# Expert MLP on one core: x of two experts loaded as 32 long rows, b1 from ScalarE, the first cast shared by two engines

## The chip, the core and the metric

One Trainium2 chip, one core. The metric is the time of one execution on the device, in microseconds (us). The runs of the kernel before took 181.45, 181.69 and 182.16 us; the median is 181.69. One further execution was recorded by the hardware profiler, and the lines below are from it.

## What is computed

Eight experts, each a two-layer perceptron on its own 256 rows of x. Everything comes in and goes out as fp32.

```python
def reference(x, w1, w2, b1, b2):   # x 8x256x512, w1 8x512x2048, w2 8x2048x512
    h = np.matmul(x, w1) + b1[:, np.newaxis, :]
    h = np.maximum(h, 0)
    return (np.matmul(h, w2) + b2[:, np.newaxis, :]).astype(np.float32)
```

One expert's w1 and w2 are 4 MB each in HBM, its x 512 KB and its result 512 KB.

## The kernel before

**Layout.** Weights and most of x are narrowed to fp16 by the DMA that loads them, which is issued by GpSimd. On the chip w1 of an expert is a tile of 128 partitions x 8192 fp16 (16 KB per partition), and so is w2. The contraction runs over partitions: rows of w1 are dealt out so that partition p holds rows 4p to 4p+3. x must therefore be transposed, and VectorE does that in blocks of 32x32 (`transposes`, lines 95 to 112): from a tile of rows t it writes xT, 128 partitions x (4 x 256) fp16. How many rows of x lie in one partition, R, decides the shape: with R = 2 an expert takes 16 instructions of 256 elements per partition (L109), with R = 4 it takes 16 of 256 (L112), with R = 8 it takes 8 of 512 (L112).

**Two products.** `first_product` (L114) makes 16 blocks of h transposed: for each, four matmuls (L121) into a PSUM tile `ph`, three of which exist, then ScalarE adds the bias from b1T and takes the maximum with 0 (L128), writing hT. In the middle of its 16 blocks it calls `transposes` for the next expert. xT has two buffers. `second_product` (L166) puts b2 into PSUM by a matmul with ones (L171), then adds 32 matmuls of hT and w2 (L178); VectorE copies one half of the result out (L156) and ScalarE the other (L157).

**Order.** The last loop (L227) runs step s = 0 to 10. At step s it puts in the DMAs that are due, runs the first product of expert s and the second product of expert s - 3 (LAG). All matmuls and all GpSimd DMAs are kept in program order. GpSimd's queue begins with w1 of expert 0, b2, b1, w1 of expert 1, x of experts 2 and 3, w1 of expert 2; the next, w1 of expert 3, must wait until the first product of expert 0 has given back its buffer, for w1 and w2 have three buffers each. From then on each load waits for such a buffer: w1 of expert 4 for the first product of expert 1, and so on. Results of experts 0 to 3 and of 4 and 5 are collected in two tiles and stored at the end by GpSimd; those of 6 and 7 are stored by SyncE and ScalarE.

**The start, which the change edits** (L187 to L211). x of experts 0 and 1 is not narrowed by its DMA. SyncE loads each as fp32 into a tile x32 of 128 partitions with two rows each (4 KB per partition), taken from the pool of result tiles. VectorE casts each to fp16 (L201), and after the first cast it transposes expert 0 (L109). b1 is loaded by GpSimd as 32 rows of 2 KB, and VectorE's four transposes at L208 make b1T out of it. They depend on b1's landing and stand, in VectorE's order, after seven of the sixteen transposes of expert 1. ScalarE's first instruction is the loading of its function table, followed by the first L128, which needs b1T.

Of the kernel before, what the change touches and what calls it, by code (L numbers as in the profile page):

```python
# [10 lines left out]
def kernel(  # L11
# [9 lines left out]
    nc = tc.nc  # L21
    fp32 = mybir.dt.float32
    fp16 = mybir.dt.float16
    E, T, H = x.shape
    M = w1.shape[2]
    P = 128
    nTB = T // P
    nKC = H // P
    nJ = M // P
    B = 32  # L30
    nB = P // B
# [9 lines left out]
    nXF32 = 2  # L41
    X_LOADS = {2: 2, 4: 4}

    def ordered(ins):
        return tc.keep_in_program_order(ins)
# [3 lines left out]
    w2_pool = ctx.enter_context(tc.tile_pool(name="w2", bufs=3))  # L49
    x_pool = ctx.enter_context(tc.tile_pool(name="xp", bufs=1))  # L50
# [3 lines left out]
    out_pool = ctx.enter_context(tc.tile_pool(name="outp", bufs=2))  # L54
# [5 lines left out]
    b1_rows = singles.tile([E * nB, M // nB], fp32)  # L60
    b1T = singles.tile([P, nJ * B + nB - 1], fp32)

    x16 = [None] * E
# [18 lines left out]
    def load_w1(e):  # L82
        w1_sb[e] = w1_pool.tile([P, nKC, M], fp16, tag="w1", name="w1sb")
        ordered(nc.gpsimd.dma_start(  # L84
            out=w1_sb[e], in_=w1[e].rearrange("(p kc) m -> p kc m", kc=nKC)
        ))
# [8 lines left out]
    def transposes(e):  # L95


        t, p0, R = x16[e]
        n = R // nTB
        xT[e] = xT_pool.tile([P, nKC, T], fp16, tag="xT", name="xT")  # L100
        for g in range(T // R // B):
            src = t[p0 + B * g : p0 + B * (g + 1)]
            for b in range(nB):
                block = src[:, :, b * (H // nB) : (b + 1) * (H // nB)].rearrange(
                    "p (n tb) (i kc) -> p tb kc n i", tb=nTB, kc=nKC)
                out = xT[e][b * B : (b + 1) * B].rearrange(
                    "p kc (tb g i n) -> p tb g kc n i", tb=nTB, i=B, n=n)
                if n == 1:
                    nc.vector.transpose(out=out[:, :, g, :, 0, :], in_=block[:, :, :, 0, :])  # L109
                    continue  # L110
                for tb in range(nTB):
                    nc.vector.transpose(out=out[:, tb, g], in_=block[:, tb])  # L112
# [71 lines left out]
                    ))  # L184
        store(e, po)

    x32 = []  # L187
    for e in range(nXF32):
        x32.append(out_pool.tile([P, nTB, H], fp32, tag="out", name="x32"))
        nc.sync.dma_start(out=x32[e], in_=x[e].rearrange("(p tb) h -> p tb h", tb=nTB))  # L190
    load_w1(0)
    ordered(nc.gpsimd.dma_start(  # L192
        out=b2_sb,
        in_=b2.rearrange("e h -> (e h)").rearrange("(o f) -> o f", o=1),
    ))
    ordered(nc.gpsimd.dma_start(out=b1_rows, in_=b1.rearrange("e (b i) -> (e b) i", b=nB)))  # L196
    nc.vector.memset(ones1, 1.0)  # L197

    for e in range(nXF32):
        t = x_pool.tile([P, nTB, H], fp16, tag=f"x{e}", name=f"x{e}")  # L200
        nc.vector.tensor_copy(out=t, in_=x32[e])  # L201
        x16[e] = (t, 0, nTB)
        if e == 0:
            transposes(e)


    for b in range(nB):
        nc.vector.transpose(  # L208
            out=b1T[b * B : (b + 1) * B, nB - 1 - b : nB - 1 - b + nJ * B],
            in_=b1_rows.rearrange("r (i j) -> r j i", j=nJ),  # L210
# [55 lines left out]
```

## Time and profile before

| what | value |
|---|---|
| median of three runs | 181.69 us |
| span of the profiled execution (no other time of it is given) | 179.7 us |
| median of the runs less that span | 2.0 us |
| TensorE matmuls busy | 129.1 us, 72% |
| VectorE busy | 88.0 us, 49% |
| ScalarE busy | 70.2 us, 39% |
| DMA | 40.56 MB landed or stored, mean 226 GB/s; 71.39 MB read from HBM, 4.19 MB written |
| GpSimd's queue (q0) | 3232 packets, 38.35 MB |
| SyncE's queue (q1) | 476 packets, 1.70 MB |
| ScalarE's queue (q10) | 112 packets, 0.39 MB |
| the two x32 loads | 512 KB each, issued at 0.74 and 1.17 us, landed 3.5 and 4.3 us after issue |
| first w1 load | issued at 1.25 us, landed 14.0 us later |
| b1 load | issued at 2.41 us, landed 13.2 us later |

How to read it: the span is cut into 40 slices of about 4.5 us, and a digit is the busy share of an engine in tenths. A matmul's end is modelled, since matmuls are pipelined. DMA bytes are counted on the side where a packet lands, so that a weight load that reads 4 MB counts as 2 MB. An instruction's line is that of the listing above. In a time line "idle before" is the time an engine stood still ahead of the instruction, with what ended the wait behind the arrow.

The start, by the time line: VectorE casts x of expert 0 at 4.26, transposes it from 5.11 to 12.29, casts x of expert 1 at 12.32, and transposes b1 from 16.19 to 20.37. TensorE begins at 15.28, when the first w1 has landed, and stops at 18.05, with all three PSUM tiles full, until ScalarE has b1T; it goes on at 22.28.

### The profile page before, as it was taken

How to read it: one execution, taken by the hardware profiler on the slowest of the kernel's cores; microseconds unless marked ns; L12 is line 12 of the kernel's file. 1: busy time of each engine (PE TensorE's matmuls, PEld its weight loads, DVE VectorE, ACT ScalarE, POOL GpSimd, SP SyncE). 2: the span in 40 equal slices, each digit the busy share in tenths (PEclk: the TensorE clock that was granted, in tenths of full speed). 3: DMA queues.
4: the chain of work that ended last, by engine and by line, in shares of the span. 5: the costliest groups of instructions: out<-in, count | busy, mean ns of one | idle time of the engine just before them, and what ended most of it. 6: DMA issues, size and time to landing. Idle time of an engine off the chain costs nothing.

```text
span 179.7 us, 1958 instructions
## 1 busy us (share of the span) xinstructions
PE 129.1 (72%) x784; PEld 85.8 (48%) x784; DVE 88.0 (49%) x125; ACT 70.2 (39%) x151; POOL 13.1 (7%) x28
## 2 busy tenths in 40 slices
PE   0005099969595970899969597969497887999950
PEld 0004079969592320795369244844195332433420
DVE  0999942987000199999999998003200020301010
ACT  0000459969593022483099005950586020020010
POOL 7000002120201010001010001000200021010000
PEclk9999999999998798589999889999999996999996
DMA  5999999999999999999999999999999999999996
GB/s 216 251 226 199 233 212 197 233 224 193 228 230 192 221 233 215 197 230 230 204 208 230 219 193 233 226 193 222 230 215 197 233 206 204 223 212 215 335 420 250
DMA packets 3829, 40.56 MB, mean 226 GB/s; under 512 B 461, under 2 KB 477, under 8 KB 1133
## 3 DMA queue, kind: packets, MB, share of 16 engines
q0 software_dynamic: 3232, 38.35, 96.6%
q1 hardware_dynamic: 476, 1.70, 2.4%
q10 hardware_dynamic: 112, 0.39, 0.5%
q8 instruction: 6, 0.10, 0.2%
q14 instruction: 3, 0.02, 0.0%
HBM read 71.39 MB, written 4.19 MB: 421 GB/s over the span
## 4 chain that ended last, share of the span: by engine, by line
DMA 66%; PE 26%; POOL 2%; another core or an unknown queue 1%; issue 1%; ACT 0%; POOLq 0%
DMA w1sb<-in_w_dram 44%; DMA w2sb<-in_w_dram 22%; PE po L178 18%; PE ph L121 8%; PE po L171 1%; POOL w1sb L84 1%; ACT out L157 0%; POOL x L76 0%; POOL b_sb L192 0%; POOL b_rows L196 0%; POOLq L250 0%
## 5 line engine op out<-in xcount | busy, mean ns | idle before, releaser
L121 PE MATMUL ph<-xT,w1sb 128*128 128x256 f16 x512 | 63.6, 289 | 34.8 <-DMA w1sb<-in_w_dram 23.9
L121 PEld LDWEIGHTS <-w1sb 128*128 128x128 f16 x512 | 59.0, 147 | 40.3 <-DMA w1sb<-in_w_dram 32.6
L178 PE MATMUL po<-w2sb,hT 128*128 128x512 f16 x256 | 61.4, 402 | 9.4 <-DMA w2sb<-in_w_dram 9.4
L112 DVE STREAM_TRANSPOSE xT<-x 32x256 f16<-32x256 f16 (+1 forms) x64 | 53.1, 889 | 25.6 <-DMA x<-in_x_dram 18.7
L128 ACT ACTIVATE hT<-ph,b1T 128x256 f16<-128x256 f32 x128 | 56.2, 474 | 13.6 <-PE ph L121 13.4
L178 PEld LDWEIGHTS <-hT 128*128 128x128 f16 x256 | 25.9, 102 | 44.7 <-issue 19.3
L156 DVE COPY out<-po 32x512 f32<-32x512 f32 (+2 forms) x22 | 15.1, 688 | 54.0 <-PE po L178 53.8
L157 ACT COPY out<-po 32x512 f32<-32x512 f32 (+2 forms) x22 | 12.7, 579 | 69.7 <-PE po L178 69.5
L109 DVE STREAM_TRANSPOSE xT<-x 32x256 f16<-32x256 f16 x32 | 14.0, 436 | 0.5
L93 POOL DMA_DIRECT2D w2sb<-in_w_dram x10 | 5.3, 534 | 72.8 <-PE po L178 72.8
L128 ACT ACT_TABLE_LOAD x1 | 1.3, 1283 | 20.5 <-DVE b1T L208 20.5
L84 POOL DMA_DIRECT2D w1sb<-in_w_dram x8 | 4.5, 558 | 63.2 <-PE ph L121 62.4
L171 PE MATMUL po<-b_sb,ones 1*128 1x512 f16 x16 | 4.8, 379 | 0.0
L208 DVE STREAM_TRANSPOSE b1T<-b_rows 32x512 f32<-32x512 f32 x4 | 4.1, 1035 | 0.1
L201 DVE CAST x<-x 128x1024 f16<-128x1024 f32 x2 | 1.5, 757 | 3.3 <-DMA x<-in_x_dram 3.3
L140 POOL DMA_DIRECT2D out_dram<-out x2 | 1.1, 542 | 10.9 <-ACT out L157 10.9
L171 PEld LDWEIGHTS <-ones 1*128 1x128 f16 x16 | 0.9, 92 | 2.1 <-issue 2.1
L76 POOL DMA_DIRECT2D x<-in_x_dram x2 | 1.1, 552 | 0.0
L197 DVE MEMSET ones<- 1x128 f16 x1 | 0.2, 165 | 0.8 <-PEq L250 0.8
L196 POOL DMA_DIRECT2D b_rows<-in_b_dram x1 | 0.5, 515 | 0.0
L192 POOL DMA_DIRECT2D b_sb<-in_b_dram x1 | 0.5, 513 | 0.0
L250 POOL MEMSET const-float32-0.0<- 128x1 f32 x1 | 0.1, 99 | 0.2 <-issue 0.2
(3 smaller groups left out, 0.3 us busy)
## 6 DMA issues: line engine op xcount, KB each, us to landing
w1sb<-in_w_dram POOLq DMA_DIRECT2D x8, 2048.0 KB, 34.5
w2sb<-in_w_dram POOLq DMA_DIRECT2D x6, 2048.0 KB, 46.8
w2sb<-in_w_dram POOLq DMA_DIRECT2D x4, 1024.0 KB, 24.0
out_dram<-out POOLq DMA_DIRECT2D x1, 2048.0 KB, 26.8
x<-in_x_dram SPq DMA_DIRECT2D x2, 512.0 KB, 3.9
x<-in_x_dram POOLq DMA_DIRECT2D x1, 1024.0 KB, 30.8
out_dram<-out POOLq DMA_DIRECT2D x1, 1024.0 KB, 17.8
x<-in_x_dram POOLq DMA_DIRECT2D x1, 512.0 KB, 24.0
```

The lines of the kernel that those rows point to most:

```text
L84: ordered(nc.gpsimd.dma_start(out=w1_sb[e], in_=w1[e].rearrange("(p kc) m -> p kc m", kc=nKC)))
L93: ordered(nc.gpsimd.dma_start(out=w2_sb[e][:, lo : lo + half], in_=src[:, lo : lo + half]))
L109: nc.vector.transpose(out=out[:, :, g, :, 0, :], in_=block[:, :, :, 0, :])
L112: nc.vector.transpose(out=out[:, tb, g], in_=block[:, tb])
L121: ordered(nc.tensor.matmul(out=ph, lhsT=w1_sb[e][:, kc, :].rearrange("p (q j) -> p q j", j=nJ)[:, :, j], rhs=xT[e][:, kc, :], start=(kc == 0),
L128: nc.scalar.activation(out=hT[e][:, j, :].rearrange("p (tb k i) -> p tb k i", tb=nTB, k=split), in_=ph.rearrange("p (tb i k) -> p tb k i", ...
L156: nc.vector.tensor_copy(out=out_sb[at : at + rows, k * nTB, :], in_=po[0][part])
L157: nc.scalar.copy(out=out_sb[at : at + rows, k * nTB + 1, :], in_=po[1][part])
L171: ordered(nc.tensor.matmul(out=t, lhsT=ones1, rhs=b2_sb[0:1, e * H : (e + 1) * H], start=True, stop=False,))
L178: ordered(nc.tensor.matmul(out=po[tb], lhsT=hT[e][:, j, tb * P : (tb + 1) * P], rhs=w2_sb[e][:, j, :], start=False, stop=(j == nJ - 1),))
L201: nc.vector.tensor_copy(out=t, in_=x32[e])
L208: nc.vector.transpose(out=b1T[b * B : (b + 1) * B, nB - 1 - b : nB - 1 - b + nJ * B], in_=b1_rows.rearrange("r (i j) -> r j i", j=nJ),)
```

## The change

SyncE loads x of experts 0 and 1 into one tile of 64 partitions, 32 for each expert, with eight rows of x (16 KB) in each partition. The tile comes from the pool of w2, not of results. ScalarE issues the load of b1 as its first instruction, in place of GpSimd. The fp16 copy is one tile x01 of the same layout. For expert 0 VectorE casts the first four rows of each partition and ScalarE the other four; expert 1 is cast by ScalarE alone. As R is now 8 for both, `transposes` takes 8 instructions of 512 elements for each, at L112, and L109 is no longer used.

```diff
-    x32 = []
+    RX = T // B
+    x32 = w2_pool.tile([nXF32 * B, RX, H], fp32, tag="w2", name="x32")
     for e in range(nXF32):
-        x32.append(out_pool.tile([P, nTB, H], fp32, tag="out", name="x32"))
-        nc.sync.dma_start(out=x32[e], in_=x[e].rearrange("(p tb) h -> p tb h", tb=nTB))
+        nc.sync.dma_start(out=x32[e * B : (e + 1) * B], in_=x[e].rearrange("(p r) h -> p r h", r=RX))
+    nc.scalar.dma_start(out=b1_rows, in_=b1.rearrange("e (b i) -> (e b) i", b=nB))
     load_w1(0)
     ordered(nc.gpsimd.dma_start(
         out=b2_sb,
         in_=b2.rearrange("e h -> (e h)").rearrange("(o f) -> o f", o=1),
     ))
-    ordered(nc.gpsimd.dma_start(out=b1_rows, in_=b1.rearrange("e (b i) -> (e b) i", b=nB)))
     nc.vector.memset(ones1, 1.0)
 
+    x01 = x_pool.tile([nXF32 * B, RX, H], fp16, tag="x01", name="x01")
     for e in range(nXF32):
-        t = x_pool.tile([P, nTB, H], fp16, tag=f"x{e}", name=f"x{e}")
-        nc.vector.tensor_copy(out=t, in_=x32[e])
-        x16[e] = (t, 0, nTB)
+        rows = slice(e * B, (e + 1) * B)
+        cut = RX // 2 if e == 0 else 0
+        if cut:
+            nc.vector.tensor_copy(out=x01[rows, :cut], in_=x32[rows, :cut])
+        nc.scalar.copy(out=x01[rows, cut:], in_=x32[rows, cut:])
+        x16[e] = (x01, e * B, RX)
         if e == 0:
             transposes(e)
```

The instructions are scheduled anew when the kernel is built. In the changed kernel VectorE's order at the start is: the memset of ones, the four transposes of b1, the cast of expert 0's half, eight transposes for expert 0, eight for expert 1, then expert 2 as before. ScalarE's is: the DMA issue, the table load, the half cast, the cast of expert 1, then the L128 blocks as before. TensorE's order is the same, and GpSimd's is the same without the load of b1.

## The prediction

> **What bounds the kernel now.** I began with the page's slices, to see which resource is never idle.
>
> ```profile
> PE   0005099969595970899969597969497887999950
> ...
> DMA  5999999999999999999999999999999999999996
> GB/s 216 251 226 199 233 212 197 233 224 193 228 230 192 221 233 215 197 230 230 204 208 230 219 193 233 226 193 222 230 215 197 233 206 204 223 212 215 335 420 250
> ```
>
> DMA is busy in all 40 slices; TensorE has gaps in most of them. The GB/s line counts bytes landed: weights arrive as fp16 at about 215, so about 430 are read, and the stores at the end run at 335 to 420 with nothing to narrow. The second view is the chain of waits, which says what the end hangs on.
>
> ```profile
> ## 4 chain that ended last, share of the span: by engine, by line
> DMA 66%; PE 26%; POOL 2%; another core or an unknown queue 1%; issue 1%; ACT 0%; POOLq 0%
> ```
> ```profile
> 4.00 34.57 DMA w1sb<-in_w_dram
> ...
> 110.12 39.38 DMA w2sb<-in_w_dram
> 149.50 0.04 issue
> 149.54 8.66 PE po L178 x32
> 158.20 0.53 PE po L171 x2
> 158.74 7.01 PE po L178 x32
> 165.75 0.53 PE po L171 x2
> 166.28 7.03 PE po L178 x32
> ```
>
> (Columns: start, duration.) The third weight load, put in at 4.00, lands at 38.57, because all that was queued before it goes first. So does w2 of expert 5: issued at 110.12, landed at 149.50. From there TensorE runs to 173.33 without a pause, and the last 512 KB store takes 4.8 us more. Whatever shifts the weight stream shifts the landing at 149.50, and with it the end, one for one. Work on VectorE or ScalarE counts only if it lets the GpSimd queue run dry.
>
> Third, the stream's first microseconds, since the change is there: the windows of half a microsecond (length, then busy time by engine, granted clock, DMA share, GB/s).
>
> ```profile
> 1.50:2.00 0.50, 0.00 (x0) 0.00 (x0) 0.00 (x0) 0.00 (x0) 0.50 (x2) 1.00 0.39 106
> 2.00:2.50 0.50, 0.00 (x0) 0.00 (x0) 0.00 (x0) 0.00 (x0) 0.50 (x2) 1.00 0.63 213
> 2.50:3.00 0.50, 0.00 (x0) 0.00 (x0) 0.00 (x0) 0.00 (x0) 0.50 (x2) 1.00 1.06 401
> 3.00:3.50 0.50, 0.00 (x0) 0.00 (x0) 0.00 (x0) 0.00 (x0) 0.50 (x2) 1.00 0.93 377
> 3.50:4.00 0.50, 0.00 (x0) 0.00 (x0) 0.00 (x0) 0.00 (x0) 0.50 (x1) 1.00 1.03 418
> 4.00:4.50 0.50, 0.00 (x0) 0.00 (x0) 0.24 (x1) 0.00 (x0) 0.50 (x2) 1.00 1.08 442
> ```
>
> These six move 0.5 x (106+213+401+377+418+442) = 978 KB. Weights can't come faster than about 215, so this is x, 1049 KB in all; the missing 70 KB at 442 take 0.16 us. **x occupies the engines from 1.5 to about 4.66, 3.16 us, and the weight stream stands behind it.**
>
> **The x load.** Bytes stay the same. 256 rows of 4 KB become 64 rows of 16 KB: on 16 engines, evenly spread, 4 packets each for 16. They go to 32 partitions per expert, 64 in all, where before each expert used 128. No row shows an uncast load to so few partitions, so I bound it. Low end: x's own best rows, 401, 377, 418 and 442, mean 410, from the first moment: 1049/410 = 2.56 us, that is 0.60 less than the 3.16 of now (the slow windows at 1.5 to 2.5 gone, with a quarter of the packets). High end: the row with packets of the same size. w1 rows are 16 KB in SBUF (128 x 8192 fp16), land at 213 GB/s at share 1.00 (window 22 to 24), and 16 of them take 262/213 = 1.23 us. Four packets per engine at that price are 4.92 us: 1.76 more than 3.16, or 2.36 more than the 2.56 of an undisturbed load. I take +1.6, near 1.76: the row with the same packet size is nearest, and a little may lie beside the first w1 packets, issued at 1.25, which can use an engine while another is held up by x. If that cover is complete, the cost is nothing.
>
> [...]
>
> **b1.** 64 KB leave the GpSimd queue, where at 426 read they cost 0.15 us, and one issue of 0.515 us goes from GpSimd. The 0.5 us by which w1 of expert 1 is put in sooner buys nothing: w1 of expert 0 is in flight until 15.28. The same 64 KB now go from ScalarE before x, while the DMA share is 0.39 or less: 0 to -0.15, taken as -0.1. ScalarE's issue (0.38 us in the ACTq row of the end) delays nothing; it did nothing until 20.45.
>
> **VectorE, ScalarE, TensorE.** New order on VectorE: memset, four b1 transposes, cast of half of x0, 8 transposes for expert 0, 8 for expert 1 (where 16 and 16 stood). They have the shape 32x512 of experts 4 to 7: 1331 ns by the grouped lines, for two of 436 before. So 8 x 1.331 = 10.6 us per expert, for 16 x 0.436 = 7.0.
> - b1 landed about as x0 does now (3.5 us after issue): 4.3. Transposes 4 x 1.035 = 4.1: 8.4.
> - x0 half on VectorE: 757 ns for 1024 elements, so 1.5 for 2048: 9.9. x0 landed meanwhile (4.3 now, plus at most 1.2).
> - ScalarE's share has no row; its 512-element copy of 579 ns, scaled, gives at most 2.3 for half of x0 and 4.6 for x1: done by 12.5, before VectorE needs either. The table load (1.28), which waited for b1T at 20.45, is done in ScalarE's idle start.
> - Transposes of x0: 20.5. The first product then runs from a cold clock: 9.78 for 64 matmuls (the product at 72.32, clock 0.50 in its first windows): ends 30.3. Now it starts at 15.28, stops at 18.05 for b1T, and ends at 30.2.
> - Transposes of x1: 31.1; second product 7.21: 38.3 (now 37.15). Transposes of expert 2: 16 of 0.43: 38.0, before its w1 lands (38.57, later by whatever x costs).
>
> So the wait for b1T goes, and longer transposes take its place; GpSimd's next loads, put in at 30.46 and 37.45 now, come at 30.4 and 38.4. The stream is covered until 38.57 by w1 of expert 2 already queued, so this is worth **0**. One wait is new: the load of w2 of expert 2 (issued at 46.65 now) needs x32's buffer, free since 12.5; behind it on GpSimd stand all later loads, none of which is held up. Out tiles no longer share with x32; nobody waits there.
>
> **Sum.** 179.7 + 1.6 - 0.1 = 181.2 of span. The page's execution has no time of its own beside its span; the median of the runs, 181.69, lies 2.0 above. 181.2 + 2.0 = **183.2 us**, 0.8% slower.
>
> **Rivals.**
> 1. *x's slowness is hidden, or isn't there.* While one engine writes x slowly, others read w1, or 16 KB rows land as fast as 4 KB ones. For it: x and w1 do overlap (4.50 to 5.00 shows 631 GB/s, more than either alone in any other window here). Against it: x has the engines nearly to itself before about 4.5. It decides if x costs under 0.9 us. Time: 179.7 + 0 to 0.8 + 2.0, about 181.8.
> 2. *The head of the stream gets shorter.* Mechanism: fewer packets fill the windows at 1.5 to 2.5 (lost there: 0.39 and 0.63 of full share, 0.5 us), at most -0.60, b1 -0.15. It decides if the early windows rise to 400 GB/s. Time: 179.7 - 0.75 + 2.0 = 180.95; to count as faster it must gain over 0.9, which even the whole of this doesn't reach, unless packets also cost less later.
> 3. *The GpSimd queue runs dry near 36.* If the first product ends late, w1 of expert 3 is issued late. Place: the load now issued at 30.46. w1 of expert 2 lands at 38.57; from an issue to full flow about 3 us pass (1.25 to about 4.5 for the first w1, beside x), so it costs from about 35 on, 1 us per us. My path says 30.4; it would need 5 us more, such as b1 landing at 9. For it: b1 stands in front of everything on VectorE. Against it: it is issued first, on a queue of its own. Time with 2 us dry: 185.2.
> 4. *The change doesn't shorten VectorE's start at all*: that is already in my sum, and worth nothing.
>
> **How the numbers follow.** Forecast (x costs 0.9 to 2.6): 0.58, at 183.2. Rival 1: 0.31. Rival 2: 0.06, of which 0.04 beyond 0.5%. Rival 3: 0.05. About 0.5% (0.91 us) is what a measurement here can tell from no change: faster 0.04, same 0.33 (rival 1 and the rest of rival 2), slower 0.63. The range leaves out rival 3, most of rival 2 and the last of the others: from 181.4 (-0.3) to 184.3 (+2.6: the +2.36 bound and 0.2 for the spread of runs). The forecast's own range is 182.6 to 184.3.
>
> **What would show it.** In windows of 0.5 us the x phase at about 213 GB/s instead of 400, reaching to 5.5 or later; the landings of w1 of expert 2 (38.57) and w2 of expert 5 (149.50) both later by the same 1 to 2 us, with the chain behind them unchanged; 32x512 transposes at 1.33 us; a first product that starts once, near 20.5, and ends near 30.3; ScalarE's casts over by 12.5. It is wrong if x is in by 4.7 and the two landings stay (rival 1), if they come sooner (2), or if a window between 34 and 40 has little DMA (3).

## The result, and the profile after

The changed kernel takes **183.54 us** (median of five runs, 183.39 to 183.72) against 181.69: a ratio of 1.0098, 95% interval 1.0084 to 1.0112. The forecast was 183.2, slower by 0.8%. The profiled execution has a span of 181.7 us, 2.0 more than before; its own time is 183.54.

First the chain of waits of the changed kernel (start, duration), beside the one of before.

```profile
3.48 37.05 DMA w1sb<-in_w_dram
40.53 0.03 issue
...
112.15 39.56 DMA w2sb<-in_w_dram
151.72 0.04 issue
151.76 8.65 PE po L178 x32
160.40 0.53 PE po L171 x2
160.94 7.01 PE po L178 x32
167.95 0.53 PE po L171 x2
168.48 7.03 PE po L178 x32
```

w1 of expert 2 lands at 40.53 in place of 38.57 (+1.96), w2 of expert 5 at 151.72 in place of 149.50 (+2.22), and everything behind it has its old length. The time was lost ahead of 40 us and never came back. The time line shows that it was lost much sooner: the first w1 lands at 17.36, before at 15.28 (+2.08).

Next the windows of half a microsecond in the head of the stream (DMA share and GB/s are the last two columns).

```profile
1.50:2.00 0.50, 0.00 (x0) 0.00 (x0) 0.00 (x0) 0.50 (x1) 0.50 (x2) 1.00 1.68 426
2.00:2.50 0.50, 0.00 (x0) 0.00 (x0) 0.00 (x0) 0.47 (x1) 0.50 (x2) 1.00 0.28 98
2.50:3.00 0.50, 0.00 (x0) 0.00 (x0) 0.00 (x0) 0.00 (x0) 0.50 (x2) 1.00 0.94 217
3.00:3.50 0.50, 0.00 (x0) 0.00 (x0) 0.00 (x0) 0.00 (x0) 0.50 (x2) 1.00 1.67 373
3.50:4.00 0.50, 0.00 (x0) 0.00 (x0) 0.00 (x0) 0.00 (x0) 0.50 (x2) 1.00 0.21 41
4.00:4.50 0.50, 0.00 (x0) 0.00 (x0) 0.00 (x0) 0.00 (x0) 0.04 (x1) 1.00 1.87 373
4.50:5.00 0.50, 0.00 (x0) 0.00 (x0) 0.00 (x0) 0.00 (x0) 0.00 (x0) 1.00 0.88 176
5.00:5.50 0.50, 0.00 (x0) 0.00 (x0) 0.00 (x0) 0.00 (x0) 0.00 (x0) 1.00 0.48 98
```

A packet counts whole in the window in which it starts, so 16 KB packets that start together make single windows jump; read the mean. The last six move 217, 373, 41, 373, 176 and 98 GB/s, 213 on average, where the kernel before moved about 410 from 2.5 to 4.5 us. DMA share stays high all the same (1.01 from 2.50 to 5.50, before 1.02 from 2.50 to 4.50): **the engines are busy but move half as much**. Busy share alone would not have shown the loss.

The queues from 1.50 to 6.00 us say who holds the engines: packets, MB, and the time that the packets took as a share of 16 engines. q1 is SyncE's queue and brings x, q10 is ScalarE's and brings b1, q0 is GpSimd's and brings the weights. First the kernel before, then the changed one:

```profile
q1 hardware_dynamic: 288, 1.05, 60.8%
q0 software_dynamic: 22, 0.36, 39.0%
```
```profile
q1 hardware_dynamic: 78, 1.02, 101.1%
q10 hardware_dynamic: 48, 0.07, 7.7%
```

Before, x takes 60.8% of 4.5 us, 2.7 us of all 16 engines. In the changed kernel it takes 4.5 us and not all of it has started by 6.00; no weight packet has started by then.

The other engines, from the time line of the start:

```profile
5.85 1.90 ACT L205 CAST x<-x 32x2048 f16<-32x2048 f32 x1 [3.38 <-DMA x<-in_x_dram]
6.20 4.15 DVE L212 STREAM_TRANSPOSE b1T<-b_rows 32x512 f32<-32x512 f32 x4 [5.22 <-DMA b_rows<-in_b_dram]
8.49 3.60 ACT L205 CAST x<-x 32x4096 f16<-32x4096 f32 x1 [0.75 <-DMA x<-in_x_dram]
...
21.53 8.96 PE L121 MATMUL ph<-xT,w1sb 128*128 128x256 f16 x64 [21.53 <-DVE xT L112]
...
30.79 0.54 POOL L84 DMA_DIRECT2D w1sb<-in_w_dram  x1 [26.75 <-PE ph L121]
```

x of expert 0 lets ScalarE start at 5.85, that of expert 1 at 8.49; VectorE began on x at 4.26 before. The first product no longer stops for b1T, but begins at 21.53, when its x has been transposed, and GpSimd puts in w1 of expert 3 at 30.79, practically where it did (30.46).

### The profile page after: what moved, and what is told of

It is laid out like the page before. It is cut to its first block, busy times and chain, and to the rows that moved or that the text cites. A ratio compares the mean times of both kernels' runs of the same rounds, so it can differ in the third digit from the quotient of the medians.

```text
span 181.7 us, 1944 instructions
## 1 busy us (share of the span) xinstructions
PE 127.7 (70%) x784; PEld 85.2 (47%) x784; DVE 93.5 (51%) x108; ACT 75.8 (42%) x153; POOL 12.5 (7%) x27
## 4 chain that ended last, share of the span: by engine, by line
DMA 67%; PE 22%; issue 5%; POOL 1%; another core or an unknown queue 1%; ACT 0%; POOLq 0%
DMA w1sb<-in_w_dram 45%; DMA w2sb<-in_w_dram 22%; PE po L178 17%; PE ph L121 4%; PE po L171 1%; POOL w1sb L84 1%; ACT out L157 0%; POOL x L76 0%; POOL b_sb L193 0%; POOLq L84 0%; POOLq L254 0%; POOLq L93 0%
## 5 line engine op out<-in xcount | busy, mean ns | idle before, releaser
L121 PE MATMUL ph<-xT,w1sb 128*128 128x256 f16 x512 | 62.2, 285 | 38.2 <-DVE xT L112 29.1
L112 DVE STREAM_TRANSPOSE xT<-x 32x512 f16<-32x512 f16 (+1 forms) x80 | 72.9, 977 | 20.6 <-DMA x<-in_x_dram 18.8
L121 PEld LDWEIGHTS <-w1sb 128*128 128x128 f16 x512 | 58.4, 146 | 42.8 <-DMA w1sb<-in_w_dram 34.8
L128 ACT ACTIVATE hT<-ph,b1T 128x256 f16<-128x256 f32 x128 | 56.3, 474 | 25.0 <-PE ph L121 24.7
L205 ACT CAST x<-x 32x2048 f16<-32x2048 f32 (+1 forms) x2 | 5.5, 2750 | 4.1 <-DMA x<-in_x_dram 4.1
L204 DVE CAST x<-x 32x2048 f16<-32x2048 f32 x1 | 1.2, 1214 | 0.0
```

The source lines that it names most:

```text
L121: ordered(nc.tensor.matmul(out=ph, lhsT=w1_sb[e][:, kc, :].rearrange("p (q j) -> p q j", j=nJ)[:, :, j], rhs=xT[e][:, kc, :], start=(kc == 0),
L128: nc.scalar.activation(out=hT[e][:, j, :].rearrange("p (tb k i) -> p tb k i", tb=nTB, k=split), in_=ph.rearrange("p (tb i k) -> p tb k i", ...
L204: nc.vector.tensor_copy(out=x01[rows, :cut], in_=x32[rows, :cut])
L205: nc.scalar.copy(out=x01[rows, cut:], in_=x32[rows, cut:])
```

## The experiments

Theory A: the loss comes from where x is written, too few of the 128 partitions at a time. Theory B: it comes from the size of the packets, 16 KB. Theory C: it comes from b1, the casts or the transposes. Differences are to the kernel before, run on the same chip for each group (medians 181.61 to 181.66). The last column is the difference of medians; it can differ by some 0.2 us from what the ratio gives, as for the two kernels with x1_high in their names.

| kernel | x written to, in rows of | median, us | ratio (95% interval) | more than before, us |
|---|---|---|---|---|
| x_wide_rest_changed | 128, 4 KB | 181.78 | 1.0006 (0.9997 to 1.0015) | 0.17 |
| x_wide_8k_rows | 128, 8 KB | 181.66 | 1.0004 (0.9995 to 1.0013) | 0.05 |
| x1_narrow_only | expert 0: 128; expert 1: 32, 16 KB | 182.11 | 1.0026 (1.0015 to 1.0037) | 0.45 |
| x0_narrow_only | expert 0: 32, 16 KB; expert 1: 128 | 182.35 | 1.0042 (1.0029 to 1.0055) | 0.69 |
| x_narrow_4k_runs | 32 per expert, 4 KB | 182.61 | 1.0052 (1.0037 to 1.0067) | 0.95 |
| x1_high_partitions_from_act | 32 per expert, apart, two queues | 183.02 | 1.0064 (1.0039 to 1.0089) | 1.36 |
| x_narrow_alone | 32 per expert, 16 KB | 183.24 | 1.0087 (1.0073 to 1.0100) | 1.63 |
| x1_high_partitions | 32 per expert, apart | 183.34 | 1.0081 (1.0051 to 1.0112) | 1.68 |
| x_16_rows_at_a_time | 16 at a time, 16 KB | 187.30 | 1.0310 (1.0290 to 1.0330) | 5.64 |

**Undoing one half, doing one half.** x_wide_rest_changed is the changed kernel with the old load, and with the old fp16 tiles and transposes, which go with the load's layout:

```diff
...
-    x32 = w2_pool.tile([nXF32 * B, RX, H], fp32, tag="w2", name="x32")
-        nc.sync.dma_start(out=x32[e * B : (e + 1) * B], in_=x[e].rearrange("(p r) h -> p r h", r=RX))
+        x32.append(out_pool.tile([P, nTB, H], fp32, tag="out", name="x32"))
+        nc.sync.dma_start(out=x32[e], in_=x[e].rearrange("(p tb) h -> p tb h", tb=nTB))
...
```

> The load of x is put back (128 partitions, 4 KB rows, two result tiles); b1 from ScalarE and the shared first cast stay. Theory A, the loss is in where x is written (few partitions), and theory B, it is in the size of its packets: both say the loss goes, 181.5 to 181.8, and w1 of expert 2 lands near 38.5 again. Theory C, the loss comes from b1 or from the casts and transposes: it stays near 183.5.

x_narrow_alone is the kernel before with the new load (the same lines the other way round), b1 from GpSimd and both casts on VectorE.

> The kernel before with only the load of x changed (64 partitions, 16 KB rows); b1 from GpSimd, VectorE does all casts. Theories A and B: the whole loss, 183.5 to 183.7, with w1 of expert 2 landing near 40.6. Theory C: 181.7.

The first is back at the time of before, 1.0006, with w1 of expert 2 used at 38.45; the second has 1.63 us of loss. Theory C falls for b1, the casts and the table load: b1 from ScalarE, the shared cast and the table load out of the way are worth nothing that can be measured. The transposes change together with the load in both runs, so these two don't tell them apart. Two kernels below do: x_narrow_4k_runs and x_16_rows_at_a_time have the changed kernel's transposes and lose 0.95 and 5.64 us, so the loss doesn't follow them. The difference of 0.30 between the changed kernel and x_narrow_alone is not settled, since their intervals overlap.

**Few partitions or large packets.** x_wide_8k_rows loads both experts with one DMA into all partitions, with rows twice as long as before; x_narrow_4k_runs writes the same 64 partitions as the change, in the old 4 KB.

```diff
 # x_wide_8k_rows
+    RX = nXF32 * T // P
+    nc.sync.dma_start(out=x32, in_=x[0:nXF32].rearrange("e (p r) h -> (e p) r h", r=RX))
 # x_narrow_4k_runs
...
+        to = x32[e * B : (e + 1) * B].rearrange("p (d c s) h -> p c d (s h)", d=2, c=2)
+        of = x[e].rearrange("(p c d s) h -> p c d (s h)", c=2, d=2, s=2)
+        for c in range(2):
+            nc.sync.dma_start(out=to[:, c], in_=of[:, c])
...
```

(The casts of x_narrow_4k_runs, not printed here, put the rows back in order.)

> The changed kernel, with x of both experts by one load into 128 partitions, rows of 8 KB (128 packets), 64 partitions for each expert. Theory A: no loss, 181.4 to 181.8. Theory B: packets of twice the size of before cost about a third of the loss or more, 182.3. If fewer packets help the head of the stream, as rival 2 of the prediction has it, up to 0.75 us less than before: 181.0.

> The changed kernel, with x into the same 64 partitions but in runs of 4 KB (256 packets): two loads for each expert, each writing every other pair of rows, so that no two runs touch. Theory A (few partitions): the loss stays, 183.3 to 183.8, and the window from 2 to 5 us moves about 215 GB/s. Theory B (large packets): it goes, 181.7, with 400 GB/s from 3 us on.

8 KB rows into 128 partitions cost nothing that can be measured (0.05 us), so larger packets aren't the cause by themselves. (16 KB rows into 128 partitions were not run.) x_wide_8k_rows also has its tile in the pool of w2, which is thereby not the cause either. But 4 KB runs into few partitions did not keep the whole loss, as theory A said: 0.95 of the changed kernel's 1.85. The time line of x_narrow_4k_runs says where the rest went:

```profile
6.04 1.90 ACT L210 CAST x<-x 32x2048 f16<-32x2048 f32 x1 [3.58 <-DMA x<-in_x_dram]
...
17.02 3.60 ACT L212 CAST x<-x 32x4096 f16<-32x4096 f32 x1 [9.08 <-DMA x<-in_x_dram]
```

x of expert 0 is there at 6.04, about as in the changed kernel, but expert 1 only at 17.02 (8.49 there). The queues of this kernel, first from 1.50 to 5.50, where expert 0 is loaded, then from 6.00 to 16.00, where expert 1 is:

```profile
q1 hardware_dynamic: 160, 0.52, 61.2%
```
```profile
q0 software_dynamic: 161, 1.91, 89.7%
q1 hardware_dynamic: 151, 0.49, 13.2%
```

The bytes divided by the time that they took of the 16 engines give the rate at which the engines get through such packets: 0.52 MB in 61.2% of 4 us are 213 GB/s, 0.49 MB in 13.2% of 10 us are 371 (x of the kernel before: 1.05 MB in 60.8% of 4.5 us, 384). So expert 0 pays the full price of a narrow write with 4 KB packets too, and expert 1, whose packets go between those of w1, pays almost none, though it also writes 32 partitions. Its slowness isn't hidden; it doesn't arise. By these rows a narrow write is slow ahead of the weights (213 GB/s) and not among their packets (371). That packet size matters because it decides how much of x is moved the slow way is an inference from them. (The profiled execution, 183.11, was the slowest of the four.)

**How the rate goes with the partitions.** x_16_rows_at_a_time cuts each of the change's two loads into two of 16 partitions: same 64 partitions in the end, same 64 packets.

```diff
...
+        src = x[e].rearrange("(p r) h -> p r h", r=RX)
+        for lo in range(0, B, B // 2):
+            nc.sync.dma_start(out=x32[e * B + lo : e * B + lo + B // 2], in_=src[lo : lo + B // 2])
...
```

> The changed kernel, with the load of each expert cut into two of 16 partitions: same 64 partitions, same 64 packets of 16 KB, only fewer partitions written at a time. Theory A in its strong form (the rate goes with the partitions that are written at the same time): the rate halves again, 1049 KB at about 107 GB/s are 9.8 us in place of 4.9, so 188.4. If the limit belongs to the set of 64 partitions, or to the packets (theory B): 183.3 to 183.7.

187.30 was measured, 1.1 below the strong form and far from 183.7. The queue of x while x has the engines nearly to itself, in three kernels: x_wide_8k_rows from 3.00 to 5.00, x_narrow_alone from 2.50 to 6.50, x_16_rows_at_a_time from 3.30 to 5.40.

```profile
q1 hardware_dynamic: 93, 0.76, 91.2%
```
```profile
q1 hardware_dynamic: 68, 0.79, 94.6%
```
```profile
q1 hardware_dynamic: 26, 0.26, 102.1%
```

By bytes and time as above, these are 417, 209 and 121 GB/s for 128, 32 and 16 partitions at a time: 32 have half of what 128 have, not a quarter, and 16 a good half of what 32 have. (The third is rough: it rests on 16 packets of 16 KB, the other ten are of a few bytes.)

With 16 partitions the loss goes beyond x itself, for the weights beside it are slowed too. The first w1 packets in x_16_rows_at_a_time, from 4.00 to 7.00, and those of x_wide_8k_rows, from 6.00 to 12.00:

```profile
q0 software_dynamic: 16, 0.26, 59.5%
```
```profile
q0 software_dynamic: 80, 1.31, 102.2%
```

59.5% of 3 us on 16 engines for 16 packets are 1.79 us for one; 102.2% of 6 us for 80 packets are 1.23.

**One expert at a time.** x0_narrow_only and x1_narrow_only are the kernel before with one of its two loads narrow.

```diff
 # x0_narrow_only; x1_narrow_only has the two layouts exchanged
...
+    nc.sync.dma_start(out=x32[0], in_=x[0].rearrange("(p r) h -> p r h", r=RX))
+    nc.sync.dma_start(out=x32[1], in_=x[1].rearrange("(p tb) h -> p tb h", tb=nTB))
...
```

> The kernel before with x of expert 0 alone in 32 partitions of 16 KB; expert 1 as before. Theory A without cover (the engines are held up by narrow writes whatever else is queued): half of the loss, about +0.8 to +1.0 us, 182.5. With cover by other transfers, the first load pays more than its half, since it stands alone, up to the whole: 182.5 to 183.3.

> The kernel before with x of expert 1 alone in 32 partitions of 16 KB; expert 0 as before. It runs beside the first packets of w1. Theory A without cover: half of the loss, 182.5, as for expert 0. With cover: 181.7 to 182.0, clearly less than for expert 0.

0.69 and 0.45: expert 0's is near its half of 1.63, expert 1's clearly below half, though not free as full cover would have made it. Their intervals overlap, so that the first load pays more than the second is not settled. Together they make 1.14, against 1.63 for both at once; with these intervals (0.8 to 1.7 for the sum, 1.3 to 1.8 for both) it is not shown that the two add up to less than the pair.

**Can placement mend it?** x1_high_partitions puts expert 1 into partitions 64 to 95; x1_high_partitions_from_act also issues it from ScalarE, so that the two loads are in flight together.

```diff
 # x1_high_partitions_from_act; x1_high_partitions has nc.sync for both
+    HIGH = P // nXF32
...
+        (nc.sync if e == 0 else nc.scalar).dma_start(
+            out=x32[e * HIGH : e * HIGH + B], in_=x[e].rearrange("(p r) h -> p r h", r=RX))
```

> The changed kernel, with x of expert 1 in partitions 64 to 95 in place of 32 to 63, both loads still from SyncE, one behind the other. If what counts is the 32 partitions that are written at one time, the loss stays: 183.3 to 183.7. If it is the set of partitions of both loads together, it falls by half or more: below 182.7.

> The same placement, with x of expert 1 issued by ScalarE (ahead of b1) while SyncE issues expert 0, so that both are in flight together. If each engine takes packets of the two queues in turn and in step with its neighbours, the loss stays: 183.3 to 183.7. If some write the low and others the high partitions at a time, 64 partitions share the load and it goes: 181.7 to 182.3.

One behind the other the loss stays, 1.68. From two queues it is 1.36: at 183.02 a little below the 183.3 that was expected for engines in step, and far above 182.3. The loads together reach 64 partitions in both halves. The queues from 1.50 to 6.00, where nothing but x is started, in x_narrow_alone and then in x1_high_partitions_from_act:

```profile
q1 hardware_dynamic: 80, 1.05, 105.3%
```
```profile
q1 hardware_dynamic: 33, 0.52, 49.5%
q10 hardware_dynamic: 34, 0.53, 48.8%
```

The same bytes take 98.3% in place of 105.3%, 7% less. At the start, from 1.50 to 2.50 and from 2.50 to 3.60, the engines take the two queues in turn and in step:

```profile
q1 hardware_dynamic: 16, 0.26, 107.2%
```
```profile
q10 hardware_dynamic: 16, 0.26, 94.0%
```

The first 16 packets all come from SyncE's queue, the next 16 all from ScalarE's, so that they write 32 partitions at a time though two loads are in flight. Later they are out of step (from 3.60 to 5.00 start 16 packets of the one and 9 of the other) and yet no faster, 1.16 us a packet for 1.07 and 1.03 in the first two windows; so the step alone doesn't explain it, and why two halves don't help stays open. Whether the 0.3 us between the two placements are real is open, since their intervals overlap. No version tried beats the kernel before: the DMA share is 9 tenths in nearly every slice, and none of these edits takes bytes away.

## Why the prediction was right

- **The bound.** "Whatever shifts the weight stream shifts the landing at 149.50, and with it the end, one for one" held: +2.08 at the first landing, +2.22 at w2 of expert 5, +2.0 at the end of the span, +1.85 in the medians.
- **The x load**, +1.6. Measured by itself: +1.63. Its price was taken from the row of a 16 KB weight packet (1.23 us, 213 GB/s), and x ran at 209. That this row fitted was partly luck. A weight packet writes 16 KB but reads 32; 8 KB of x in x_wide_8k_rows take 0.31 us (91.2% of 2 us on 16 engines, 93 packets), by which 32 KB would take 1.25, an estimate that is near its 1.23. An x packet reads only 16 KB; its slowness goes with the 32 partitions written at a time (209 GB/s, against 417 for 128). The prediction names them beside the row, as what no row shows; they were the reason, and the row a good price for the wrong one. Taking 1.6 and not 1.76, for what lies beside the first w1 packets, was luck too: in x_narrow_alone no weight packet starts before 6.00. The packet time of x rose by 2.0 us (60.8% to 105.3% of 4.5 us); why the kernel lost only 1.63 is not shown.
- **b1**, -0.1: no gain is seen. x_wide_rest_changed has it with the casts, at +0.17 with an interval from -0.05 to +0.27. b1 also landed late, 5.5 us after its issue and not 3.5, for it didn't go ahead of x, as the prediction had it, but shared the engines with slow x (only packets of q1 start from 1.50 to 2.50): in x_wide_rest_changed it took 3.1. In the changed kernel b1's queue takes 7.7% of 4.5 us, 0.35 us, ahead of the first weights.
- **VectorE, ScalarE, TensorE**, 0. Right, with the times about 1 us late for b1's sake: transposes of expert 0 done at 21.5 (20.5 forecast), the second load wave at 30.79 (30.4), ScalarE's casts over at 12.1 (12.5). Most of the delay was made up by the first product, which took 8.96 and not 9.78; the granted clock from 21.50 to 31.40 is 1.00, not cold (for the product at 72.32 in the kernel before it was 0.50 up to 75.00). Twice as many elements for each transpose cost 1332 ns on average of 48, as the rows of experts 4 to 7 said. The queue of GpSimd had 10 us in hand at 30.79, until 40.53.
- **Rivals.** Cover (1) isn't seen in the changed kernel: its weights start after 6.00. The 631 GB/s that spoke for it in the prediction is no overlap but 16 KB packets that start in one window (its DMA share is 2.78). Only with small packets is there less to pay beside the weights, 0.95 for 1.85 in x_narrow_4k_runs. The shorter head (2) is worth nothing: the early windows do rise, to 426 and 98 from 106 and 213, but x_wide_8k_rows, with half as many x packets, gains nothing. The dry queue (3) did not come: DMA is at 9 tenths in every slice after the first until the last. That b1T's wait was worth nothing (4) is shown by x_wide_rest_changed.

## What to carry to other kernels

When transfers bound a kernel, look at how many partitions one transfer spans before looking at the length of its rows: 64 long rows into 32 partitions at a time moved half of what 256 short rows into 128 did (213 GB/s against 410), and the weights behind them paid for it to the last store (+2.0 us). Busy share did not show this (1.01 against 1.02); GB/s beside it did. If a narrow layout is wanted for what comes after, short runs are worth trying, provided that nobody waits for them: in x_narrow_4k_runs the 4 KB packets of expert 1 went between those of w1 at 371 GB/s, where x of the kernel before went at 384. And the wait for b1T, which x_wide_rest_changed removes, was worth nothing that can be measured there (+0.17 us), since the end hangs on the weight stream.

## What had not been expected

Cutting the same bytes into 4 KB in place of 16 KB halved the loss of the changed kernel (0.95 for 1.85 us), at the price of a landing 8.5 us later for expert 1. Weight packets beside a write into 16 partitions were slowed as well (1.79 us for 1.23). Two narrow loads into different halves of the partitions, in flight at once, were hardly better than one behind the other (1.36 for 1.68 us lost, with intervals that overlap).
